# Keeping the two split parts of a mixer's weights in HBM for the second token half

## The chip, the cores and the metric

The kernel runs on one core of one Trainium2 chip. The metric is the device time of one execution in microseconds (us). A core has TensorE (PE: matmul, and PEld, its weight loads), VectorE (DVE), ScalarE (ACT), GpSimd (POOL) and SyncE (SP), each with its own queue of instructions that run in the order in which they stand. Before the change only SP issues DMAs; with it POOL does too.

## The reference

A trunk of two layers over 1024 tokens of 1024 features, all in float32. Layer 0 mixes tokens with a recurrent block, layer 1 with forgetting attention; beside each runs a cross-attention of four heads into 256 memory tokens. Then come an output projection and a squared-ReLU MLP.

```python
for layer in range(DEPTH):
    h = rms_norm(x, norm_mix[layer])
    if layer % N_MIXERS == 0:
        y_mix, xq = rglru_group(h, w_in_a[j], ...)   # proj = h @ w_in: u, gate, xq
    else:
        y_mix, xq = fox_group(h, w_in_b[j], ...)     # proj = h @ w_in: q, k, v, f, xq
    y_mem = memory_group(xq, mem, ...)
    x = x + jnp.concatenate([y_mix, y_mem], axis=-1) @ w_out[layer]
    x = x + sqrelu_mlp(rms_norm(x, norm_mlp[layer]), w_mlp_in[layer], w_mlp_out[layer])
```

## The kernel before

**Split weights.** Each float32 matrix product is made of three matmuls on rounded parts: a weight W is split into hi (W rounded, written by ACT) and lo (W minus hi, by DVE or POOL), an activation likewise, and the kernel adds hi·hi, hi·lo and lo·hi. `_wpart` is one such split of a piece of a tile. "Split" means this throughout.

**Weight tiles.** `self.plan` lists all weight tiles in the order of use. An entry is a source in HBM, a width (1024 columns, 512 KB; or 512 columns, 256 KB, a "half tile") and a number of pieces: 1 for tiles made by `plan_st`, 4 for tiles made by `plan_mv`. `_wraw` has SP load a tile into one of two raw buffers (`wr`), `_wsplit` splits it into one of three hi buffers (`wh`) and three lo buffers (`wl`); tile i uses buffer i mod 3. So tile i can be written when the last matmul of tile i-3 has run, and it must be there at its own first matmul. `pool_parts` says which of four pieces have their lo made by POOL; in the second token half of layer 1 it is all four.

**Two token halves.** Tokens are worked on in two halves of 512. In the mixers a weight tile is used for the first half, and much later the same tile is loaded and split again for the second. These are 60 entries: `wxqa` x4 and `wina` x8 (input projections of layer 0), `wout0` as 16 half tiles (output projection of layer 0), `wxqb` x4, `wkb`/`wqb` x8 and `wvb` x4 (projections of layer 1), `wout1m` x8 and `wout1x` x8 half tiles (output projection of layer 1). The MLP uses each weight once for both halves, and is not touched.

**Consumers.** `proj_T` uses one tile at a time (24 matmuls of 512 columns), `outproj` and `outproj2` a half tile (12 of 512 columns). `tok_proj` uses a pair of tiles: for each of four groups of 128 tokens 12 matmuls of 256 columns on the first tile of the pair, then 12 on the second, into one of two PSUM tiles `pspj`. A pair is asked for with `wpair`, which splits up to the tile behind the pair (`_wsplit(i + 3)`); so the second tile of each pair is written last, when the pair before is nearly used up.

**Order.** Python emits the instructions and weaves attention work between projections at fixed rates (`weave`); a scheduler of the framework then sets the order of each engine by its own estimate of times. Stores and loads of the residual stream (`xspill`) and of x stand on SP in the same queue as the weight loads. In the trace the second uses stand at 138 to 237 us (`wxqa`, `wina`), 305 to 353 (`wout0` halves), 1212 to 1402 (`wxqb`, `wkb`, `wqb`, `wvb`), 1455 to 1492 (`wout1m`) and 1535 to 1558 (`wout1x`); the first uses of the same at 5 to 138, 237 to 305, 1071 to 1180, 1180 to 1212 (`wout1m`) and 1411 to 1447 (`wout1x`).

Of the kernel before, what the change touches and what calls it, by code (L numbers as in the profile page):

```python
# [10 lines left out]
F32 = mybir.dt.float32  # L11
F32R = mybir.dt.float32r
# [7 lines left out]
P = 128  # L20
# [119 lines left out]
class Builder:  # L140
# [107 lines left out]
    def _wsplit(self, upto):  # L248
        nc = self.nc
        while self.wload < min(len(self.plan), upto):  # L250
            i = self.wload
            self._wraw(i + 1)
            n = self.plan[i][1]
            parts = self.plan[i][2]
            raw = self._wrawbuf(i)
            hi, lo = (self._wbuf(i, b) for b in (self.whi, self.wlo))
            if parts in ("s1", "s2"):
                G, q = nc.gpsimd, 256
                a11, a12, a22, a21 = (raw[:, k * q:(k + 1) * q] for k in range(4))
                f = self.F.get()  # L260
                if parts == "s1":
                    self.wx = f
                    G.tensor_tensor(f[:, q:2 * q], a21, a22, ALU.add)
                    G.tensor_tensor(f[:, 0:q], f[:, q:2 * q], a11, ALU.subtract)
                    self._wpart(hi[:, 0:512], lo[:, 0:512], raw[:, 0:512], nc.vector)
                    self._wpart(hi[:, 512:1024], lo[:, 512:1024], f[:, 0:512], nc.vector)
                else:
                    G.tensor_tensor(f[:, 0:q], a11, a21, ALU.subtract)
                    G.tensor_tensor(f[:, q:2 * q], a12, self.wx[:, 0:q], ALU.subtract)
                    self._wpart(hi[:, 512:768], lo[:, 512:768], a22, nc.vector)  # L270
                    self._wpart(hi[:, 0:512], lo[:, 0:512], f[:, 0:512], nc.vector)
# [184 lines left out]

    def plan_kv(self, l, idx=range(8)):
        for c in idx:
            self.plan.append((self.ins["wkv"][l * 8 + c], 1024, 4))

    def kv(self, l):
        nc = self.nc
# [574 lines left out]
    def plan_fox(self, c):  # L1037
        for w in ("wkb", "wqb"):
            self.plan_mv(w, (2 * c, 2 * c + 1))
        for kk in range(2):  # L1040
            self.plan.append((self.ins[f"wvb{c}"][kk], 1024 if c else 1056, 4))

    def fox_proj(self, h, c):
        nc = self.nc
# [222 lines left out]
    def run(self):  # L1267
        self.xs = self.dr.tile([8, P, S], F32, name="xspill")
        nc = self.nc
        xT = self.ins["xT"]  # L1270
        K_M, K_X, K_0, K_1 = [4, 5, 6, 7], [0, 1, 2, 3], [0, 1], [2, 3]

        self.plan.append((self.ins["wina"][0], 1024, 4))
        self.plan_st("wina", range(1, 4))
        for m in range(4):
            self.plan_kv(0, (2 * m, 2 * m + 1))
# [2 lines left out]
        self.plan_mv("wxqa")  # L1279
        self.plan_st("wina", range(8))  # L1280
        self.plan_st("wout0", range(8))
        w0 = self.ins["wout0"]
        self.plan += [(w0[m, :, 0:512], 512, 1) for m in range(7)]
        self.plan += [(w0[m, :, 512:1024], 512, 1) for m in range(7)]
        self.plan += [(w0[7, :, 0:512], 512, 1), (w0[7, :, 512:1024], 512, 1)]
        self.plan_mlp(0, 0, 0)
        self.plan_kv(1)
        self.plan_mv("wxqb")
        self.plan_fox(0)
        self.plan_fox(1)  # L1290
        self.plan += [(self.ins["wout1m"][m], 512, 1) for m in range(8)]
        self.plan_mv("wxqb")
        self.plan_fox(0)
        self.plan_fox(1)
        self.plan += [(self.ins["wout1x"][m], 512, 1) for m in range(8)]
        self.plan += [(self.ins["wout1m"][m], 512, 1) for m in range(8)]
        self.plan += [(self.ins["w1"][32 + m], 1024, 1) for m in range(TUNE["nz"])]
        self.plan += [(self.ins["wout1x"][m], 512, 1) for m in range(8)]
        self.plan_mlp(1, TUNE["nz"], TUNE["nw"])


        nrm = [self.norm_split_first(0, "gmix0", xT), self.norm_split(1, "gmix0", xT, True)]
# [231 lines left out]
```

## Time and profile before

| | |
|---|---|
| median of 3 runs | 2215.03 us (2212.84 to 2220.73) |
| the profiled execution | 2215.74 us, its span 2214.1 us |
| busy PE / DVE / ACT / POOL | 97% / 73% / 42% / 44% of the span |
| mean granted TensorE clock | 0.986 |
| moved by DMA | 307.85 MB, 139 GB/s on average |

Busy time is the share of the span in which an engine worked on an instruction. A wait is put down to the engine whose work came last. The granted clock is 1.00 at 2.4 GHz and 0.5 at 1.2 GHz; a value between is a mean over a stretch.

### The profile page before, as it was taken

To read this page: it belongs to the slowest core of one execution; us is meant where nothing else is said; L and a number is where in the kernel's file an instruction comes from. 1 tells how busy PE (TensorE), PEld (TensorE's weight loads), DVE (VectorE), ACT (ScalarE), POOL (GpSimd) and SP (SyncE) were. 2 spreads that over 40 slices of the span, in tenths; PEclk is the share of its full clock that TensorE was granted. 3 is DMA by queue.
4 is the path that set the end of the run, shared out by engine and by line. 5 is a ranking of instruction groups with operands and counts; after the bars stand their busy time and mean duration, and the time that the engine had idled before them with its cause. 6 is when DMAs were issued, how large, how long until landed. Compare 5 with 4: busy or idle time off the path is not lost. (4 is left out here: it accounts for less than half of the span.)

```text
span 2214.1 us, 31106 instructions
## 1 busy us (share of the span) xinstructions
PE 2138.4 (97%) x10662; PEld 1780.2 (80%) x10662; DVE 1617.9 (73%) x2991; ACT 932.4 (42%) x1852; POOL 983.2 (44%) x952
## 2 busy tenths in 40 slices
PE   7889999999999999998999998999999999999999
PEld 6788777888888888876998997777778888888887
DVE  8997776666666666669677877986787566576667
ACT  5755634222232222334556856765433223232222
POOL 3742421545545545456142452331364454454454
PEclk9989999999999999999999998999999999999999
DMA  5412254435445345345425221364564354354353
GB/s 177 129 58 67 93 178 157 134 123 190 138 129 190 130 136 183 126 134 166 125 87 172 96 73 49 125 193 129 168 209 167 104 187 159 107 190 151 108 194 128
DMA packets 138782, 307.85 MB, mean 139 GB/s; under 512 B 15552, under 2 KB 17664, under 8 KB 138624
## 3 DMA queue, kind: packets, MB, share of 16 engines
q1 hardware_dynamic: 138624, 305.87, 42.9%
q8 instruction: 84, 1.38, 0.3%
q14 instruction: 74, 0.61, 0.1%
HBM read 225.03 MB, written 80.77 MB: 138 GB/s over the span
## 5 line engine op out<-in xcount | busy, mean ns | idle before, releaser
L301 PE MATMUL pspj<-r,wh 128*128 128x512 f32 x2656 | 845.8, 398 | 15.5 <-ACT wh L245 5.6
L301 PEld LDWEIGHTS pspj<-r,wh 128*128 128x128 f32 x2656 | 498.4, 189 | 137.3 <-ACT wh L245 5.6
L301 PE MATMUL pspj<-r,wl 128*128 128x512 f32 x1328 | 528.4, 398 | 0.2 <-DVE wl L246 0.2
L245 ACT ACTIVATE wh<-wr 128x256 fp32r<-128x256 f32 (+3 forms) x497 | 275.3, 581 | 391.1 <-PE pspt L923 194.7
L246 DVE TENSOR_TENSOR wl<-wr,wh 128x256 fp32r<-128x256 f32 (+2 forms) x386 | 303.7, 794 | 67.7 <-ACT wh L245 66.7
L371 ACT ACTIVATE r<-f 128x512 fp32r<-128x512 f32 x250 | 156.8, 631 | 416.7 <-POOL f L881 278.4
L881 POOL TENSOR_TENSOR f<-f 128x512 f32<-128x512 f32 x128 | 167.6, 1310 | 320.0 <-DVE f L880 317.3
L301 PEld LDWEIGHTS pspj<-r,wl 128*128 128x128 f32 x1328 | 251.2, 189 | 60.9 <-DVE wl L246 0.7
L301 PE MATMUL pspj<-wh,r 128*128 128x256 f32 (+1 forms) x1408 | 275.5, 290 | 15.2 <-ACT f L450 5.1
L372 DVE TENSOR_TENSOR r<-f,r 128x512 fp32r<-128x512 f32 x250 | 190.3, 773 | 132.8 <-ACT r L371 132.6
L923 PE MATMUL pspt<-r,wh 128*128 128x512 f32 x768 | 246.8, 395 | 1.2 <-ACT f L948 1.0
L301 PEld LDWEIGHTS pspj<-wh,r 128*128 128x128 f32 x1408 | 225.9, 193 | 19.8 <-ACT f L450 6.0
L301 PE MATMUL pspj<-wl,r 128*128 128x256 f32 (+1 forms) x704 | 201.8, 288 | 5.0 <-DVE wl L246 5.0
L960 POOL TENSOR_TENSOR f<-f,f 128x512 f32<-128x512 f32 x64 | 96.3, 1505 | 230.8 <-DVE f L959 218.5
L923 PEld LDWEIGHTS pspt<-r,wh 128*128 128x128 f32 x768 | 144.1, 188 | 36.5 <-ACT wh L245 1.4
L923 PE MATMUL pss<-r,wh 128*128 128x512 f32 x512 | 161.6, 396 | 3.5 <-DVE f L968 3.5
L923 PE MATMUL pspj<-r,wh 128*128 128x512 f32 x512 | 161.2, 396 | 1.4 <-DVE f L949 1.2
L923 PE MATMUL pspt<-r,wl 128*128 128x512 f32 x384 | 152.4, 397 | 0.9 <-DVE wl L246 0.9
L246 POOL TENSOR_TENSOR wl<-wr,wh 128x256 fp32r<-128x256 f32 (+2 forms) x111 | 89.7, 831 | 132.5 <-ACT wh L245 129.0
L301 PEld LDWEIGHTS pspj<-wl,r 128*128 128x128 f32 x704 | 135.5, 193 | 6.7 <-DVE wl L246 5.8
L245 ACT ACTIVATE wh<-f 128x512 fp32r<-128x512 f32 x128 | 80.4, 630 | 143.2 <-PE pspj L923 61.3
L880 DVE SCALAR_TENSOR_TENSOR f<-pspj,f 128x512 f32<-128x512 f32 x128 | 87.7, 687 | 66.4 <-PE pspj L301 66.1
(273 smaller groups left out, 3635.5 us busy)
## 6 DMA issues: line engine op xcount, KB each, us to landing
f<-xspill SPq DMA_DIRECT2D x312, 256.0 KB, 3.0
xspill<-f SPq DMA_DIRECT2D x288, 256.0 KB, 3.0
wr<-in_w_dram SPq DMA_DIRECT2D x134, 512.0 KB, 4.1
f<-in_xT_dram SPq DMA_DIRECT2D x32, 256.0 KB, 3.7
wr<-in_wkv_dram SPq DMA_DIRECT2D x16, 512.0 KB, 3.9
wr<-in_wina_dram SPq DMA_DIRECT2D x15, 512.0 KB, 3.8
f<-cscr SPq DMA_DIRECT2D x24, 256.0 KB, 3.5
wr<-in_wxqa_dram SPq DMA_DIRECT2D x8, 512.0 KB, 3.8
```

Of the source, the lines that this page charges most:

```text
L245: self.nc.scalar.activation(hi, raw, AF.Copy)
L246: eng.tensor_tensor(lo, raw, hi.bitcast(F32), ALU.subtract)
L301: self.nc.tensor.matmul(out, lhsT=a, rhs=b, start=(j == 0), stop=(j == n - 1))
L371: self.nc.scalar.activation(hi[:, :n], src, AF.Copy)
L372: self.nc.vector.tensor_tensor(lo[:, :n], src, hi[:, :n].bitcast(F32), ALU.subtract)
L880: nc.vector.scalar_tensor_tensor(r[:, n], ps, 0.0, self.rsb[h][:, n], ALU.max, ALU.mult)
L881: nc.gpsimd.tensor_tensor(r[:, n], r[:, n], r[:, n], ALU.mult)
L923: nc.tensor.matmul(ps, lhsT=a, rhs=b, start=(j == 0), stop=(j == 5))
L960: G.tensor_tensor(c12, c12, u, ALU.add)
```

## The change

`share` goes over the plan. A full tile that is used again gets two tiles of its size in HBM (`wsp`, for hi and lo). At its first use, after the split, SP stores hi and lo there (104 stores: 36 tiles and 16 half tiles of two parts each). At its second use nothing is loaded to `wr` and nothing is split: POOL issues two DMAs, which bring hi and lo from HBM straight to the `wh` and `wl` buffers (120 DMAs for 60 entries). The 16 half tiles of `wout0` take their halves of the eight full tiles stored at the first use.

```diff
+    def ent(self, name, i, n, parts, a=0):
+        return (self.ins[name][i][:, a:a + n], n, parts, (name, i), a)
+
+    def share(self):
+        own, keep = {}, {}
+        for j, e in enumerate(self.plan):
+            if len(e) < 5:
+                continue
+            k, full = e[3], self.ins[e[3][0]].shape[2]
+            if k in own:
+                if k not in keep:
+                    keep[k] = [self.dr.tile([P, full], F32R, name=self.nm("wsp")) for _ in range(2)]
+                self.plan[j] = (None, e[1], "ld", k, e[4])
+            elif e[1] == full:
+                own[k] = j
+        self.own = {j: keep[k] for k, j in own.items() if k in keep}
+        self.keep = keep
...
-            if parts in ("s1", "s2"):
+            if parts == "ld":
+                _, _, _, k, a = self.plan[i]
+                for b, d in zip((hi, lo), self.keep[k]):
+                    nc.gpsimd.dma_start(b, d[:, a:a + n])
+            elif parts in ("s1", "s2"):
...
+                for b, d in zip((hi, lo), self.own.get(i, ())):
+                    nc.sync.dma_start(d.bitcast(F32), b.bitcast(F32))
...
-            self.plan.append((self.ins["wkv"][l * 8 + c], 1024, 4))
+            self.plan.append(self.ent("wkv", l * 8 + c, 1024, 4))
...
-        self.plan += [(w0[m, :, 0:512], 512, 1) for m in range(7)]
-        self.plan += [(w0[m, :, 512:1024], 512, 1) for m in range(7)]
-        self.plan += [(w0[7, :, 0:512], 512, 1), (w0[7, :, 512:1024], 512, 1)]
+        self.plan += [self.ent("wout0", m, 512, 1, a) for a in (0, 512) for m in range(7)]
+        self.plan += [self.ent("wout0", 7, 512, 1, a) for a in (0, 512)]
...
+        self.share()
```

The scheduler orders the engines anew. Three places show it. The first is PE in the second token half of layer 1, at the second tile of the pair `wqb` (the buffers `wh2_153` and `wl2_156`; the first tile of the pair is in `wh1_152` and `wl1_155`). Before, the 12 matmuls of a token group on the first tile are followed by its 12 on the second:

```order
L301 MATMUL pspj_840_11226<-wh1_152,r22_88 128x256
L301 MATMUL pspj_840_11226<-wl1_155,r22_88 128x256
L301 MATMUL pspj_840_11226<-wh1_152,r23_89 128x256
L301 MATMUL pspj_840_11226<-wh2_153,r18_84 128x256
L301 MATMUL pspj_840_11226<-wl2_156,r18_84 128x256
```

In the order of the change, the same place (`pspj_944` is the group that was `pspj_840`, and `pspj_946` the next group, in the other PSUM tile):

```order
L327 MATMUL pspj_946_11336<-wh1_152,r1_67 128x256
L327 MATMUL pspj_946_11336<-wh1_152,r22_88 128x256
L327 MATMUL pspj_946_11336<-wl1_155,r22_88 128x256
L327 MATMUL pspj_946_11336<-wh1_152,r23_89 128x256
L327 MATMUL pspj_944_11301<-wh2_153,r18_84 128x256
L327 MATMUL pspj_944_11301<-wl2_156,r18_84 128x256
```

The next group's 12 matmuls on the first tile moved ahead of the second tile's first matmul, and attention work moved between. From the last matmul of the buffer's old tile to the first on the new one there stood 24 matmuls of 256 columns and 3 of 128; now there stand 38 of 256, 12 of 128, 2 of 384 and 2 of 512.

The second place is POOL in the same stretch (`f` tiles times `frc` are softmax rows, `xr` the scaling of queries). Before:

```order
L1185 TENSOR_SCALAR f_127<-f_127,frc_10998 128x384
L246 TENSOR_TENSOR wl_156<-wr_150,wh_153 128x256
L1185 TENSOR_SCALAR f_144<-f_144,frc_11016 128x512
L246 TENSOR_TENSOR wl_156<-wr_150,wh_153 128x256 x2
L246 TENSOR_TENSOR wl_154<-wr_149,wh_151 128x264 x4
L246 TENSOR_TENSOR wl_155<-wr_150,wh_152 128x264 x4
```

In the order of the change:

```order
L1211 TENSOR_SCALAR f_127<-f_127,frc_11101 128x384
L280 DMA wl_156<-wsp_224 128x1024
L280 DMA wh_153<-wsp_223 128x1024
L1211 TENSOR_SCALAR f_144<-f_144,frc_11119 128x512
L280 DMA wl_154<-wsp_226 128x1056
L280 DMA wh_151<-wsp_225 128x1056
L280 DMA wl_155<-wsp_228 128x1056
L280 DMA wh_152<-wsp_227 128x1056
```

Four lo pieces of a tile became two DMA issues at the same place in POOL's queue.

The third place is SP where the half tiles `wout1m` are used first. Before:

```order
L241 DMA wr_149<-in_wout1m_dram 128x512
L794 DMA xspill<-f_127 128x512
L241 DMA wr_150<-in_wout1m_dram 128x512
L794 DMA xspill<-f_134 128x512
L241 DMA wr_149<-in_wout1m_dram 128x512
L400 DMA f_134<-xspill 128x512
```

In the order of the change:

```order
L261 DMA wr_149<-in_wout1m_dram 128x512
L302 DMA wsp_247<-wh_153 128x512
L820 DMA xspill<-f_127 128x512
L302 DMA wsp_248<-wl_156 128x512
L261 DMA wr_150<-in_wout1m_dram 128x512
L302 DMA wsp_249<-wh_151 128x512
L820 DMA xspill<-f_134 128x512
L302 DMA wsp_250<-wl_154 128x512
L261 DMA wr_149<-in_wout1m_dram 128x512
L426 DMA f_134<-xspill 128x512
```

Two stores of parts now stand ahead of each weight load, and so ahead of the `xspill` loads and stores that follow.

## Rows read from the trace of the kernel before

**Rows 1.** The page: span, and busy us (share) of each engine.

```profile
span 2214.1 us, 31106 instructions
...
PE 2138.4 (97%) x10662; PEld 1780.2 (80%) x10662; DVE 1617.9 (73%) x2991; ACT 932.4 (42%) x1852; POOL 983.2 (44%) x952
```

**Rows 2.** Waits of PE: for whom, us in total, times, longest.

```profile
PE pspj L301 <- ACT wh L245: 5.6, 1, 5.6
PE pspj L301 <- DVE wl L246: 5.2, 4, 2.7
PE pspj L301 <- ACT f L450: 5.1, 4, 1.9
PE pspt L301 <- DVE wl L246: 4.6, 1, 4.6
```

**Rows 3.** Stretches: us, busy (instructions) by engine, PE clock, DMA share, GB/s.

```profile
core 0: us, PE busy (x) PEld busy (x) DVE busy (x) ACT busy (x) POOL busy (x), PEclk, DMA share, GB/s
64.00:138.00 74.00, 61.03 (x375) 55.57 (x374) 70.24 (x123) 49.82 (x106) 48.90 (x42) 0.86 0.32 93
138.00:237.00 99.00, 97.13 (x584) 84.87 (x583) 77.38 (x159) 55.43 (x120) 32.04 (x40) 1.00 0.23 70
237.00:305.00 68.00, 60.81 (x267) 48.92 (x266) 56.18 (x82) 38.90 (x76) 30.27 (x27) 0.92 0.42 134
305.00:328.00 23.00, 21.46 (x96) 16.90 (x95) 12.48 (x28) 7.31 (x13) 2.69 (x2) 1.00 0.58 187
328.00:353.00 25.00, 25.00 (x109) 20.19 (x108) 19.03 (x29) 14.90 (x23) 0.00 (x0) 1.00 0.68 215
1071.00:1180.00 109.00, 109.00 (x906) 107.88 (x905) 77.53 (x221) 60.77 (x165) 36.16 (x46) 1.00 0.30 91
1180.00:1212.00 32.00, 31.52 (x168) 26.22 (x166) 22.39 (x55) 18.27 (x43) 7.49 (x11) 1.00 0.62 181
1212.00:1238.00 26.00, 21.74 (x143) 19.39 (x144) 20.92 (x54) 21.55 (x55) 8.37 (x13) 0.93 0.47 163
1238.00:1345.00 107.00, 104.46 (x853) 102.30 (x853) 80.80 (x235) 65.95 (x185) 55.75 (x84) 1.00 0.26 78
1448.00:1493.00 45.00, 41.97 (x227) 34.57 (x226) 39.15 (x104) 30.37 (x69) 15.66 (x20) 1.00 0.61 187
1535.00:1559.00 24.00, 23.49 (x102) 18.34 (x101) 19.51 (x29) 13.57 (x23) 1.04 (x1) 1.00 0.50 171
```

**Rows 4.** Groups by shape, ACT, DVE, POOL: the splits (busy us, mean ns, idle before).

```profile
L245 ACT ACTIVATE wh<-wr 128x256 fp32r<-128x256 f32 x276 | 101.2, 410 | 66.3 <-PE pspt L923 22.9 <-DMA wr<-in_wkv_dram 17.6 <-PE pspj L301 15.6
L245 ACT ACTIVATE wh<-wr 128x1024 fp32r<-128x1024 f32 x93 | 98.5, 1059 | 166.8 <-PE pspt L923 111.9 <-PE pspj L301 28.7 <-DMA wr<-in_w_dram 17.8
L245 ACT ACTIVATE wh<-wr 128x512 fp32r<-128x512 f32 x112 | 70.3, 629 | 158.1 <-PE pspj L301 72.6 <-PE pspt L923 59.9 <-DMA wr<-in_wout1x_dram 7.4
...
L246 DVE TENSOR_TENSOR wl<-wr,wh 128x1024 fp32r<-128x1024 f32 x93 | 123.8, 1332 | 18.3 <-ACT wh L245 18.2
...
L246 DVE TENSOR_TENSOR wl<-wr,wh 128x512 fp32r<-128x512 f32 x111 | 87.9, 792 | 30.4 <-ACT wh L245 30.0
...
L246 POOL TENSOR_TENSOR wl<-wr,wh 128x256 fp32r<-128x256 f32 x98 | 79.5, 832 | 121.1 <-ACT wh L245 117.6 <-PE pspt L1210 3.4
```

**Rows 5.** The page: DMA queue share, and issues (count, KB, median us to landing).

```profile
q1 hardware_dynamic: 138624, 305.87, 42.9%
...
f<-xspill SPq DMA_DIRECT2D x312, 256.0 KB, 3.0
...
wr<-in_w_dram SPq DMA_DIRECT2D x134, 512.0 KB, 4.1
...
wr<-in_wxqa_dram SPq DMA_DIRECT2D x8, 512.0 KB, 3.8
```

**Rows 6.** DMA view: half tiles of layer 1's output projection.

```profile
wr<-in_wout1m_dram SPq DMA_DIRECT2D x16, 256.0 KB, 2.9
```

**Rows 7.** Waits of ACT from 1205 to 1230 us.

```profile
ACT r L365 <- DMA f<-xspill: 5.2, 4, 2.0
```

More of the change, by code (lines that the diff above doesn't have):

```diff
@@ L642, in plan_st @@
         for i in idx:
-            self.plan.append((self.ins[name][i], 1024, 1))
+            self.plan.append(self.ent(name, i, 1024, 1))
     def plan_mv(self, name, idx=range(4)):
         for i in idx:
-            self.plan.append((self.ins[name][i], 1024, 4))
+            self.plan.append(self.ent(name, i, 1024, 4))
     def proj_T(self, xs, tag="pj"):
@@ L1040, in plan_fox @@
         for kk in range(2):
-            self.plan.append((self.ins[f"wvb{c}"][kk], 1024 if c else 1056, 4))
+            self.plan.append(self.ent(f"wvb{c}", kk, 1024 if c else 1056, 4))
     def fox_proj(self, h, c):
@@ L1271, in run @@
         K_M, K_X, K_0, K_1 = [4, 5, 6, 7], [0, 1, 2, 3], [0, 1], [2, 3]
-        self.plan.append((self.ins["wina"][0], 1024, 4))
+        self.plan.append(self.ent("wina", 0, 1024, 4))
         self.plan_st("wina", range(1, 4))
@@ L1281, in run @@
         self.plan_st("wout0", range(8))
-        w0 = self.ins["wout0"]
-        self.plan += [(w0[m, :, 0:512], 512, 1) for m in range(7)]
-        self.plan += [(w0[m, :, 512:1024], 512, 1) for m in range(7)]
-        self.plan += [(w0[7, :, 0:512], 512, 1), (w0[7, :, 512:1024], 512, 1)]
+        self.plan += [self.ent("wout0", m, 512, 1, a) for a in (0, 512) for m in range(7)]
+        self.plan += [self.ent("wout0", 7, 512, 1, a) for a in (0, 512)]
         self.plan_mlp(0, 0, 0)
@@ L1290, in run @@
         self.plan_fox(1)
-        self.plan += [(self.ins["wout1m"][m], 512, 1) for m in range(8)]
+        self.plan += [self.ent("wout1m", m, 512, 1) for m in range(8)]
         self.plan_mv("wxqb")
@@ L1294, in run @@
         self.plan_fox(1)
-        self.plan += [(self.ins["wout1x"][m], 512, 1) for m in range(8)]
-        self.plan += [(self.ins["wout1m"][m], 512, 1) for m in range(8)]
+        self.plan += [self.ent("wout1x", m, 512, 1) for m in range(8)]
+        self.plan += [self.ent("wout1m", m, 512, 1) for m in range(8)]
         self.plan += [(self.ins["w1"][32 + m], 1024, 1) for m in range(TUNE["nz"])]
-        self.plan += [(self.ins["wout1x"][m], 512, 1) for m in range(8)]
+        self.plan += [self.ent("wout1x", m, 512, 1) for m in range(8)]
         self.plan_mlp(1, TUNE["nz"], TUNE["nw"])
+        self.share()
         nrm = [self.norm_split_first(0, "gmix0", xT), self.norm_split(1, "gmix0", xT, True)]
```

## The prediction

> **What bounds the kernel now.** I read the page first, then the waits of PE, then a table of stretches of the mixers. PE is busy for 97% of the span, DVE for 73%, ACT and POOL for under half [rows 1]. So only what PE waits for can be won back: 2214.1 - 2138.4 = 76 us in all. The waits of PE say on whom: of the splits only a few, 5.6 us for hi (the start of the program), 5.2 and 4.6 us for lo [rows 2]. The lo waits lie nearly all between 64 and 138 us, where DVE works 70.2 of 74 us [rows 3]. That is a first use, and the change leaves its split as it is.
>
> The stretches of the second uses are the ones to price. PE idles there 99.0 - 97.1 = 1.9 us (138 to 237), 1.5 (305 to 328), 0 (328 to 353), 4.3 (1212 to 1238), 2.5 (1238 to 1345), 3.0 (1448 to 1493) and 0.5 (1535 to 1559): 13.7 us together [rows 3]. The clock is 1.00 in all but one of them: 0.93 from 1212 to 1238, worth 0.07 x 26 = 1.8 us. So about 15.5 us is the most that the change can give.
>
> **What is removed.** By the plan 60 splits go: on ACT 32 pieces of 512 columns at 0.629 us, 8 of 1024 at 1.059, 80 of 256 at 0.410, about 61 us; on POOL 62 lo pieces of about 0.83, 51 us (counted in the two orders); on DVE 32 at 0.79, 8 at 1.33 and 18 short ones, some 45 us [rows 4]. All of it lies beside PE's work. It pays only where ACT or DVE is what PE waits for. I take 2 us of the 4.3 at 1212 to 1238, 2 of the 3.0 at 1448 to 1493 and 1 of the 1.5 at 305 to 328: **-5**, with bounds 0 and -15.5.
>
> **What is added: the reloads.** A tile is now two DMAs that POOL issues when the buffer's old tile is used up. Most have room: counted in the changed order, PE has 10 to 20 us of matmuls between the old tile's last and the new one's first for `wina` and for the first tile of most pairs. Room is short at the second tile of a pair. A matmul of 256 columns costs PE 109.0/906 = 0.12 us, one of 512 25.0/109 = 0.229 [rows 3]; I take 0.06 for 128 and 0.172 for 384 in proportion. At `wqb`'s second tile the order before leaves 24 x 0.12 + 3 x 0.06 = 3.1 us, the changed one 38 x 0.12 + 12 x 0.06 + 2 x 0.172 + 2 x 0.229 = 6.1 us. The nine places of this kind, in program order, have 4.5, 6.5 (`wxqa`), 6.8 (`wxqb`), 6.7, 6.1, 5.8, 6.5, 4.8 and 7.5 us (`wkb` to `wvb`). The scheduler has made room, but not much.
>
> The price of a reload is not in the trace, since nothing is issued from POOL. The nearest row is a 512 KB load from SP: 3.8 to 4.1 us to landing [rows 5]. The second part shares the engines with the first: 305.87 MB in 42.9% of 2214.1 us is 322 GB/s with all engines busy [rows 5], so 0.524 MB more is 1.6 us. For POOL's work on an issue I take that of a short POOL piece, 0.83 us [rows 4], twice. Together 4.0 + 1.6 + 1.6 = 7.2 us. Below, the second part and the issues could cost nothing: 4.1. Above, one part after the other: 2 x 4.1 + 2 x 0.83 = 9.9. I take 7.2, since transfers in flight together are what the kernel's SP loads do all the time. Against the nine rooms that leaves 2.7 + 0.7 + 0.4 + 0.5 + 1.1 + 1.4 + 0.7 + 2.4 + 0 = **+9.9** us; at 4.1 nothing; at 9.9 it is 33.9.
>
> The Trainium skill (DMA: Bandwidth & Descriptors, Anatomy of one DMA) gives a DMA issued from GpSimd about 2.0 us plus its bytes at 436 GB/s, so an estimate of 4.4 us for both parts issued together. By that estimate this term would be 0. No row here has a DMA from POOL, and for the same bytes the rows from SP are slower than this formula (3.8 to 4.1 us against 3.2), so I keep the rows.
>
> Half tiles: two parts cost 2.9 [rows 6] + 0.8 + 1.6 = 5.3 us. PE has 12 x 0.229 x 2 = 5.5 us between for some 20 of the 32, which just covers it, more for the others, and 3.2 us for one `wout1x` tile: **+2**. At the upper price of 2 x 2.9 + 1.7 = 7.5 us three buffers give a tile each (7.5 + 2.75)/3 = 3.4 us in place of 2.75, so 20 x 0.67 = 13 us.
>
> A POOL DMA that waits for PE's last matmul holds POOL's queue; behind it stand softmax rows (`frc`) for the attention's transposes. Before, the lo pieces stood in the same places and waited for the same release, so this is new only as far as PE itself is late. Nothing is added for it.
>
> **What is added: the stores.** 36 x 2 x 0.524 + 16 x 2 x 0.262 = 46 MB go out, and 46 MB of reloads come in, in place of 23 MB of loads. Taken as engine time at 322 GB/s: from 1071 to 1180, 16 tiles of 1.05 MB are 52 us of 109, which makes a DMA share of 0.30 + 0.48 = 0.78; from 237 to 305, 8.4 MB are 26 us of 68: 0.42 + 0.38 = 0.80; from 1180 to 1212, 4.2 MB are 13 us of 32: 0.62 + 0.41 = 1.03; and the reloads' extra 0.26 MB for nine half tiles from 328 to 353 make 0.68 + 0.29 = 0.97 [rows 3]. Two stretches are full. An excess of 0.03 x 32 is 1 us; the loads behind it on SP's queue are those of the residual stream, for which ACT waits 5.2 us already from 1205 to 1230 [rows 7]. I take **+2**, with bounds 0 and 13: at the upper one each of eight pairs of stores holds up the loads behind it for its own 0.52 MB, 1.6 us. Elsewhere the cover is the 0.2 and more of idle DMA share; if it were gone, the same 1.6 to 3.3 us a tile would show.
>
> **The clock.** Where PE idles 7.2 us with waits of 3.4 and 3.2 us, from 237 to 305, the granted clock is 0.92, between its two levels of 1.2 and 2.4 GHz, which costs 0.08 x 68 = 5.4 us; in stretches with 1.5 to 3.0 us of idle time it stays at 1.00 [rows 3]. Two of the new stalls are over 2 us. I take **+2**; were all 33.9 us to come, 5.4/7.2 of it would be 25.
>
> **The sum.** -5 + 9.9 + 2 + 2 + 2 = +11 on the profiled execution's own 2215.74 us (span 2214.1; the median of the runs is 2215.03, so it is a usual one): 2226.7 against it, 2226 against the median.
>
> **The rivals.**
> *The reload is dear.* One part comes after the other, or POOL is slow to issue: 9.9 us and 7.5 us. Then +33.9 + 13, with 2 to 13 for stores and about half of the clock's upper bound, less 5: 2262 to 2285, or some 2250 if only the full tiles suffer. For it speaks that no row shows POOL doing this; against, that the scheduler left 5 to 7 us where 3 to 4 stood. It decides from 8 us on. The Trainium skill (SBUF — State Buffer, Who interferes with whom) adds that GpSimd cannot write descriptors while DVE runs a one-source copy or scalar operation in SBUF. No run here shows it yet. As a mechanism of this kernel, an issue that has to let one DVE instruction end first waits 0.8 to 1.3 us, as long as DVE's pieces are [rows 4]: nine times at most 12 us, so some 2238, which the forecast's own range holds.
> *The cover holds, nothing is won.* A reload takes 6 us or less; what ACT and DVE no longer do was hidden. Sum -2 to +2: 2213 to 2218. For it speaks PE's 97%.
> *Faster.* Reloads fit as in the last case, and PE's idle time in the second uses goes with the splits: up to -15.5 + 2, so 2202. It is decided from 1212 to 1238, where ACT works 21.6 of 26 us and DVE 20.9 [rows 3]; the waits there must be for ACT's queue. Against it: part of them is for the residual stream [rows 7], which the stores make later.
> *The stores hold SP.* +13 from 1180 to 1238 and some as much again from 237 to 305, where each store pair is 1.05 MB: 2235 to 2245, with reloads fitting.
>
> **Chances.** Forecast (2214 to 2240) 0.42; dear reload 0.18; nothing won 0.17; faster 0.13; stores 0.10. A measurement of this kernel tells about 0.5%, 11 us, from no change: faster means under 2204, slower over 2226. Half of the forecast's case lies beyond that line: slower 0.21 + 0.18 + 0.10 = 0.49; same 0.21 + 0.15 = 0.36; faster 0.13 + 0.02 = 0.15. The range 2202 to 2262 leaves out the dear half of the first rival and the best end of the third, under 2 in 10.
>
> **What would show it.** In the changed profile: ACT and POOL busy time down by some 61 and 50 us, and DVE's by 45. PE waits for POOL DMAs into `wh` or `wl` at the second tiles of pairs, most at `wxqa` and the last `wqb` pair. The time from issue to landing in the list of DMA issues is the price itself: under 5 us for 512 KB, the nine stalls are gone; over 8, the first rival holds. The stretch from 1180 to 1238 shows the stores: a DMA share near 1 and longer waits for `xspill`. I am wrong if PE's waits do not change and the time still does, or if the attention's work, which the scheduler moved into the gaps, makes PE wait for DVE in new places.

## The result and the profile after

| | before | changed |
|---|---|---|
| median of 20 runs each | 2215.12 us (2212.46 to 2220.73) | 2219.34 us (2215.00 to 2226.76) |
| ratio, 95% interval | | 1.0019 [1.0012, 1.0025] |
| span of the profiled execution | 2214.1 us | 2220.3 us |

The change costs 4.2 us, 0.2%. That is on the side that was forecast, inside the range and 6.7 us under the forecast of 2226; it lies within the 0.5% that the prediction called no change. The profiled execution lost 6.2 us.

The head of the changed kernel's page, span and busy times, answers to [rows 1]:

```profile
span 2220.3 us, 31077 instructions
...
PE 2136.6 (96%) x10662; PEld 1775.3 (80%) x10662; DVE 1566.7 (71%) x2933; ACT 881.8 (40%) x1732; POOL 1006.5 (45%) x1010
```

DVE is down by 51 us and ACT by 51, POOL is up by 23, and PE's own work is the same to 2 us. So the 6 us, and two more, are idle time of PE: span less busy time is 75.7 us before and 83.7 now. Which waits of PE are new (engine, line, waited for: us in total, times, longest) answers to [rows 2]:

```profile
PE pspj L327 <- ACT wh L265: 7.7, 3, 5.6
...
PE pspt L1236 <- DVE r L1169: 5.0, 1, 5.0
...
PE pspj L327 <- ACT r L397: 2.7, 1, 2.7
...
PE pss L844 <- DMA wl<-wsp: 1.7, 1, 1.7
PE pspj L844 <- DMA wh<-wsp: 1.4, 1, 1.4
...
PE pspj L327 <- DMA wh<-wsp: 0.6, 1, 0.6
```

The reloads themselves (`wsp`) stop PE for 1.7 + 1.4 us at half tiles of `wout0` and 0.6 us at the last pair of `wvb`, 3.7 us in all. Two other waits, of 5.0 and 2.7 us, each happen once. Where they are, a table of stretches of the changed kernel tells; it is cut where PE has done the same work as at 138.5, 236.6, 304.9 us and so on in the trace before, and one row (1204 to 1222) is a close-up. It answers to [rows 3]:

```profile
core 0: us, PE busy (x) PEld busy (x) DVE busy (x) ACT busy (x) POOL busy (x), PEclk, DMA share, GB/s
135.20:233.60 98.40, 95.89 (x578) 83.74 (x577) 68.08 (x147) 46.76 (x108) 36.22 (x54) 1.00 0.44 148
233.60:302.00 68.40, 60.81 (x268) 48.60 (x267) 55.55 (x80) 36.05 (x71) 34.23 (x32) 0.93 0.69 234
302.00:366.00 64.00, 59.29 (x260) 47.06 (x259) 27.02 (x51) 18.22 (x27) 18.27 (x30) 1.00 0.79 243
1072.00:1181.00 109.00, 108.20 (x897) 106.87 (x896) 76.84 (x218) 60.59 (x165) 36.23 (x46) 1.00 0.68 242
1181.00:1210.50 29.50, 29.50 (x154) 24.73 (x152) 19.22 (x49) 14.64 (x34) 6.82 (x13) 1.00 0.90 294
1204.00:1222.00 18.00, 10.96 (x57) 8.90 (x56) 9.59 (x23) 7.09 (x16) 4.21 (x8) 0.86 1.06 352
1210.50:1265.30 54.80, 44.89 (x324) 42.27 (x323) 33.44 (x92) 34.88 (x81) 12.32 (x22) 0.91 0.50 167
1265.30:1351.00 85.70, 85.69 (x696) 83.87 (x695) 57.81 (x194) 37.95 (x105) 30.87 (x51) 1.00 0.46 144
1351.00:1404.70 53.70, 49.02 (x280) 39.77 (x278) 44.97 (x138) 39.68 (x98) 18.44 (x28) 0.90 0.17 55
...
1497.20:1535.00 37.80, 37.31 (x189) 30.52 (x187) 23.11 (x47) 19.13 (x39) 13.68 (x16) 1.00 0.61 198
1535.00:1563.80 28.80, 25.71 (x105) 19.92 (x104) 18.82 (x28) 13.50 (x22) 6.41 (x11) 0.94 0.56 162
```

From 1265.3 to 1351 us, where five of the nine feared tiles stand, PE is idle for 0.01 us; before, the same work (1258.0 to 1344.1) had 2.5 us of idle time. From 1210.5 to 1265.3, the four tiles of `wxqb`, PE idles 9.9 us and the clock is 0.91; before, this took 47.0 us (1211.0 to 1258.0), 4.4 of them idle, at 0.96. That is 7.8 us lost in one place. From 1535 to 1563.8 PE idles 3.1 us at 0.94; before, it was 23.6 us with 0.3 us idle: 5.2 us more. The stretch ahead of it takes 37.8 us where it was 42.1 (1492.5 to 1534.6), 4.3 us less, so that the two together lose 0.9.

**What holds PE at 1212 us.** Rows of the changed kernel's timeline, ACT, DVE and PE (start us, us, engine, line, in brackets the idle time before and what ended it):

```profile
1214.28 0.72 ACT L391 ACTIVATE r<-f,par 128x512 fp32r<-128x512 f32 x1 [5.85 <-DMA f<-xspill]
1215.03 0.68 ACT L1168 ACTIVATE r<-pspt,gk 64x512 fp32r<-64x512 f32 x1
1215.04 0.75 DVE L392 SCALAR_TENSOR_TENSOR r<-f,par,r 128x512 fp32r<-128x512 f32 x1 [5.60 <-ACT r L391]
...
1216.42 0.76 DVE L1169 SCALAR_TENSOR_TENSOR r<-pspt,gk,r 64x512 fp32r<-64x512 f32 x1
...
1217.23 0.69 PE L1236 MATMUL pspt<-ident,f 128*128 128x128 f32 x2 [5.04 <-DVE r L1169]
...
1218.22 0.72 ACT L391 ACTIVATE r<-f,par 128x512 fp32r<-128x512 f32 x1 [2.51 <-DMA f<-xspill]
...
1218.99 0.58 PE L327 MATMUL pspj<-wh,r 128*128 128x256 f32 x1 [1.07 <-ACT r L391]
```

ACT waits 5.85 us for a block of the residual stream from HBM (`f<-xspill`). Behind that wait on ACT's queue stands L1168, and behind the same block on DVE's queue L1169, both for the attention; PE waits for L1169. The waits view names DVE, but what is late is a DMA. The place of L1168 in ACT's order costs little by itself: once L1169 is done, PE has two matmuls left (0.7 us) and then stands again, for the next block of the residual stream (ACT's L391 at 1218.22), which the first projection of the second half reads. That block was issued at 1207.43 us and landed at 1218.20, after 10.8 us; in the kernel before it took 7.3 (1205.53 to 1212.81). The DMA view of 1204 to 1222 us says why (share of the 16 engines by queue, then KB each and median us from issue to landing):

```profile
q0 software_dynamic: 864, 3.15, 53.5%
q1 hardware_dynamic: 1756, 3.20, 52.7%
issues: line engine op xcount, KB each, median us to landing
wh<-wsp POOLq DMA_DIRECT2D x3, 512.0 KB, 7.2
wl<-wsp POOLq DMA_DIRECT2D x3, 512.0 KB, 8.6
f<-xspill SPq DMA_DIRECT2D x6, 256.0 KB, 9.4
```

The DMA engines are full (1.06 in the table; the share counts the time of packets, and it can pass 1). At the end of the first half of the last output projection the three weight buffers come free one after the other, POOL issues the parts of three `wxqb` tiles from 1203.7 to 1212.5 us, 3.15 MB, and just then SP fetches the residual stream for the second half. A load that lands in 3.1 us as a rule takes 9.4. The stretch was crowded before the change too; the same views of the kernel before:

```profile
1204.00:1222.00 18.00, 15.17 (x88) 12.18 (x87) 15.08 (x35) 13.07 (x32) 6.24 (x10) 1.00 0.85 268
...
f<-xspill SPq DMA_DIRECT2D x7, 256.0 KB, 6.3
```

So the loads went from 6.3 to 9.4 us here, and PE's idle time from 2.8 to 7.0. POOL's queue (q0) and SP's (q1) get half of the engines each, and a load that POOL issued later, at 1208.37 us, was in at 1215.62 although it is twice as large as the block that SP had issued at 1207.43. The Trainium skill (DMA: Bandwidth & Descriptors, Queues, rings and completion order) says that each DMA engine goes round the queues that have work, a packet at a time; 53.5% against 52.7% agrees with it.

What a reload cost, and what POOL's issues cost, from the page's list of DMA issues and from the groups by shape (these answer to [rows 5] and [rows 4]):

```profile
wl<-wsp POOLq DMA_DIRECT2D x26, 512.0 KB, 4.7
wh<-wsp POOLq DMA_DIRECT2D x26, 512.0 KB, 5.7
...
wh<-wsp POOLq DMA_DIRECT2D x32, 256.0 KB, 4.2
wl<-wsp POOLq DMA_DIRECT2D x32, 256.0 KB, 4.6
```

Of a full tile POOL mostly issues the lo part first (18 of 26, among them the nine feared ones), as here for the second tile of a pair:

```profile
1329.14 0.58 POOL L280 DMA_DIRECT2D wl<-wsp  x1 [0.83 <-PE pspj L327]
1329.72 0.54 POOL L280 DMA_DIRECT2D wh<-wsp  x1
```

So the first part lands 4.7 us after its own issue and the second 5.7 after its own; both are in 6.3 us after the first issue (median of the 26; 5.2 us for the half tiles).

```profile
L266 POOL TENSOR_TENSOR wl<-wr,wh 128x256 fp32r<-128x256 f32 x44 | 40.0, 928 | 88.1 <-ACT wh L265 80.3 <-DMA wr<-in_wvb_dram 7.7
...
L280 POOL DMA_DIRECT2D wh<-wsp x60 | 33.0, 550 | 60.5 <-PE pspj L327 35.4 <-PE pspt L844 11.3 <-PE pss L844 9.8
```

### The profile page after: what moved, and what is told of

It is laid out like the page before. It is cut to its first block, busy times and chain, and to the rows that moved or that the text cites. A ratio compares the mean times of both kernels' runs of the same rounds, so it can differ in the third digit from the quotient of the medians.

```text
span 2220.3 us, 31077 instructions
## 1 busy us (share of the span) xinstructions
PE 2136.6 (96%) x10662; PEld 1775.3 (80%) x10662; DVE 1566.7 (71%) x2933; ACT 881.8 (40%) x1732; POOL 1006.5 (45%) x1010
## 5 line engine op out<-in xcount | busy, mean ns | idle before, releaser
L265 ACT ACTIVATE wh<-wr 128x512 fp32r<-128x512 f32 (+3 forms) x377 | 218.2, 604 | 362.4 <-PE pspt L949 191.2
L397 ACT ACTIVATE r<-f 128x512 fp32r<-128x512 f32 x250 | 156.5, 631 | 423.1 <-POOL f L907 274.8
L266 DVE TENSOR_TENSOR wl<-wr,wh 128x256 fp32r<-128x256 f32 (+3 forms) x328 | 257.4, 792 | 50.3 <-ACT wh L265 49.8
L265 ACT ACTIVATE wh<-f 128x512 fp32r<-128x512 f32 x128 | 80.4, 630 | 144.5 <-PE pspj L949 64.7
L1211 POOL TENSOR_SCALAR f<-f,frc 128x512 f32<-128x512 f32 (+2 forms) x96 | 61.5, 651 | 154.1 <-DVE frc L1209 123.0
```

The costliest lines, as they stand in the source:

```text
L265: self.nc.scalar.activation(hi, raw, AF.Copy)
L266: eng.tensor_tensor(lo, raw, hi.bitcast(F32), ALU.subtract)
L397: self.nc.scalar.activation(hi[:, :n], src, AF.Copy)
L1211: nc.gpsimd.tensor_scalar(s[:, :n], s[:, :n], rc, 0.0, ALU.mult, ALU.add)
```

## The experiments

Theory A after the first look: the loss is made in the second mixer, by reloads that fill the DMA engines while the residual stream is due, and by the end of the last `wout1x` tiles. Theory B, the rival that the prediction named: the stores do it. Theory C: the split was never in the way, and only the order of the work moves the time. Fourteen kernels were run, each against the kernel before on the same chip, most with 11 runs (e2 has 5, e10 has 6). The last column is the ratio's distance from 1 times 2215 us; by it the changed kernel stands at +4.2.

| run | what goes through HBM | median us | ratio, 95% interval | in us |
|---|---|---|---|---|
| e1 | first mixer alone | 2212.67 | 0.9991 [0.9982, 1.0000] | -2.0 |
| e2 | second mixer alone | 2222.35 | 1.0036 [1.0022, 1.0050] | +8.0 |
| e3 | stores alone, nothing reloaded | 2215.87 | 1.0002 [0.9991, 1.0013] | +0.4 |
| e4 | all, a quarter of each `wxqb` part reloaded | 2208.91 | 0.9978 [0.9969, 0.9988] | -4.9 |
| e5 | all but `wxqb` | 2216.54 | 1.0005 [0.9995, 1.0015] | +1.1 |
| e6 | all but `wout1m`, `wout1x` | 2216.55 | 1.0011 [1.0002, 1.0020] | +2.4 |
| e7 | all, reloads issued by SP | 2215.69 | 1.0000 [0.9991, 1.0009] | 0.0 |
| e8 | first mixer, `wkb`, `wqb`, `wvb` | 2210.28 | 0.9979 [0.9970, 0.9987] | -4.7 |
| e9 | as e5, 16 idle POOL DMAs more | 2210.74 | 0.9978 [0.9968, 0.9989] | -4.9 |
| e10 | as e8, reloads issued by SP | 2205.72 | 0.9960 [0.9945, 0.9975] | -8.9 |
| e11 | `wxqb` alone | 2214.99 | 1.0001 [0.9991, 1.0010] | +0.2 |
| e12 | `wkb`, `wqb`, `wvb` alone | 2209.29 | 0.9974 [0.9965, 0.9983] | -5.8 |
| e13 | all, `wxqb` reloaded by SP | 2213.36 | 0.9996 [0.9987, 1.0005] | -0.9 |
| e14 | all but `wout1x` | 2213.83 | 0.9997 [0.9988, 1.0007] | -0.7 |

Where each kernel stands against the kernel before, in us, at PE's last matmul on the tile named (its time in the trace, less that of before; one execution each, and two executions of the same order differ by 2 to 3 us):

| PE's last matmul on | before, at | changed | e4 | e6 | e11 | e12 | e13 | e14 |
|---|---|---|---|---|---|---|---|---|
| `wxqa`, second use | 169.8 | -2.8 | -2.5 | -2.1 | +0.6 | +0.9 | -1.8 | -2.4 |
| `w1` tile 1, layer 0 | 378.2 | 0.0 | +2.6 | -2.8 | +2.5 | +0.4 | -3.1 | -1.5 |
| `wout1m`, first use | 1211.0 | -0.5 | +3.3 | -1.2 | +2.3 | +1.2 | -3.0 | -1.0 |
| `wxqb`, last tile, second use | 1258.0 | +7.3 | -0.1 | +3.6 | +5.0 | -2.5 | +1.8 | +7.4 |
| `wqb`, last tile, second use | 1344.1 | +6.7 | -0.4 | +4.1 | +1.0 | -3.0 | +0.7 | +7.1 |
| `wvb`, last tile, second use | 1402.5 | +2.1 | -6.9 | +0.6 | +1.3 | -8.0 | -5.1 | +2.0 |
| `w1` tile 3, early, layer 1 | 1534.6 | +0.3 | -10.7 | -0.1 | -1.5 | -10.4 | -7.8 | -1.3 |
| `wout1x`, second use | 1558.2 | +5.6 | -3.9 | -0.2 | -1.2 | -10.2 | -3.0 | 0.0 |
| the end | 2209.5 | +6.1 | -4.2 | -0.7 | +0.4 | -10.4 | -2.8 | -0.2 |

**e1 and e2: the two mixers apart.**

```diff
-            if len(e) < 5:
+            if len(e) < 5 or not (j < 60):      # e1; in e2 (j > 60)
```

> Only the weights of the first mixer (wxqa, wina, wout0) go through HBM; the second mixer splits twice as before. Theory A (the loss arises in the second mixer alone, where the first reloads of wxqb fill the DMA engines while the residual stream is due): no change, 2213 to 2217 us, since the two traces stand level again at 365 us. Theory B (the stores cost time wherever they are made): half of the loss or more shows here, 2217 us or more. Theory C (the split was never in the way and nothing but the order moves the time): within 2 us of before as well.

> Only the weights of the second mixer (wxqb, wkb, wqb, wvb, wout1m, wout1x) go through HBM. Theory A: all of the loss is here, 2218 to 2221 us, with the same 5 us gap of PE near 1215 us and the same gap near 1542 us as in the changed kernel. Theory B: about half of it, some 2217 us. If the two halves of the change depend on each other, the time is neither.

PE's order in e1 is the changed kernel's in the first mixer and the old one in the second, and the reverse in e2. The first mixer wins 2.0 us (its interval just reaches 0), the second loses 8.0: theory A has the place right, and both times fall a little outside the ranges that it gave. In e2's trace the gap of PE stands at 1219 us (5.2 us), and the one of 2.7 us at 1544.

**e3: the stores alone.**

```diff
-                self.plan[j] = (None, e[1], "ld", k, e[4])
```

> Both parts of each tile are stored at first use, and the second use loads the weights and splits them as before: 46 MB of stores are added and nothing is taken away. Theory A: the stores are hidden, 2214 to 2217 us, and PE's waits at the start of the second token half of the second mixer (1211 to 1258 us) stay as before. Theory B: the stores push the residual stream's loads back on SP's queue, 2219 us or more, with a longer wait of ACT for xspill.

46 MB of stores cost 0.4 us, with an interval from -2.0 to +2.9. From 1205 to 1240 us ACT waits 1.7 us for `xspill`, less than before [rows 7]. Theory B falls as the only cause. PE's order differs here too, in 1,712 of 10,612 matmuls, and the time does not move, which speaks against theory C as far as this order goes.

**e4: fewer bytes in the reloads of `wxqb`.**

```diff
+                c = 256 if k[0] == "wxqb" else n
                 for b, d in zip((hi, lo), self.keep[k]):
-                    nc.gpsimd.dma_start(b, d[:, a:a + n])
+                    nc.gpsimd.dma_start(b[:, :c], d[:, a:a + c])
```

> The reloads of wxqb alone fetch 256 of the 1024 columns of each part (the rest of the buffer keeps old values, so a part of the weights is left out of the computation); everything else is the changed kernel, and PE's order differs from it only in the stretch from 1206 to 1299 us. Theory A: the DMA engines are no longer full from 1204 to 1220 us, ACT waits for xspill no longer than before (5 us in place of 8), the 5 us gap of PE goes; up to 8 us less than the changed kernel where nothing later takes it back, 2211 to 2216 us. Theory B and C: 2218 to 2221 us, the gap stays.

Where the changed kernel is at +4.2 us, this one is at -4.9: 9 us go with the bytes of four tiles. The DMA engines are still busy from 1204 to 1222 us, at 0.97 (that part of the expectation was wrong), but the residual stream lands in 5.2 us and PE's longest gap there is 1.5 us:

```profile
1204.00:1222.00 18.00, 15.69 (x92) 13.30 (x91) 13.61 (x30) 10.70 (x23) 5.39 (x10) 1.00 0.97 299
```

The block that holds PE in the changed kernel stands at the same place in SP's order here and lands 5.5 us after its issue (1211.53 to 1217.01) in place of 10.8. So theory A holds for the landing. Theory C is not wholly out: PE's order is the changed kernel's except from 1206 to 1299 us (507 of 10,612 matmuls), and ACT's L1168 stands ahead of the residual blocks in e4, as it does before. By the rows at 1218 us that order is worth little, but no run separates it.

**e5 and e6: one group of tiles taken back.**

```diff
-            if len(e) < 5:
+            if len(e) < 5 or not (e[3][0] != "wxqb"):      # e5
+            if len(e) < 5 or not (not e[3][0].startswith("wout1")):      # e6
```

> wxqb alone is split twice as before; all other repeated tiles go through HBM, and the computation is whole. Theory A (reload burst): at the start of the second token half of the second mixer the loads of wxqb are half as many bytes again, PE's 5 us gap at 1215 us goes, and the 10 us that the changed kernel loses from 1211 to 1245 us mostly stay away: 2209 to 2214 us. Rival (the loss there is one of the order in which the scheduler put the work, or of POOL's queue, and not of bytes): 2217 us or more.

> wout1m and wout1x are split twice as before; the mixers' other tiles go through HBM. PE's order is that of the kernel before from 1425 us on. Theory A says nothing is won at 1215 us (the three reloads of wxqb are the same), but the 2.7 us gap near 1542 us and the slow clock behind it belong to the order of the last wout1x tiles and go: up to 5 us less than the changed kernel, 2213 to 2218 us. If the stores of wout1m ahead of 1210 us feed the burst, the gap at 1215 us shrinks too and the time is below 2212 us.

e5's median misses theory A's 2209 to 2214. Its trace says why: in e5 the `xspill` loads from 1204 to 1222 us land in 4.3 us and PE's longest gap from 1205 to 1225 us is 1.1 us; PE does its last matmul at 2206.1 us, 3.4 before the kernel before, and yet the span is 2217.4. The 11.3 us between are a last DRAIN of POOL of 10.5 us, behind which the program ends (e9). In e6 the gap near 1542 us is gone, as theory A said, and the gap of 5.0 us becomes two of 2.6, which points to a share of the stores of `wout1m`, though the order of the work differs there as well; PE ends 0.7 us ahead of the kernel before. A DRAIN of 8.6 us covers this up: the span ends 8.7 us after PE in place of 4.6.

**e9: the last DRAIN.** The kernel is e5's with one line more in the split of the MLP's tiles, taken for the first 16 of them:

```diff
+            self.nc.gpsimd.dma_start(t, f[:, 0:16])      # t: a tile in HBM, not read
```

> The kernel of e5 (wxqb split twice, all other tiles through HBM, 112 DMAs issued by POOL) and 16 DMAs more from POOL of 8 KB each (16 columns of an intermediate of the first MLP block go to a scratch tensor that nobody reads); the order of PE's instructions is that of e5 to the last one. In e5 the program does not end until a last DRAIN of POOL of 10.5 us is over, against 1.4 us without POOL DMAs and 2.5 us in the changed kernel with its 120; with 56, 64, 80, 88 and 112 it is 1.37 us + 0.082 us for each. Theory: that DRAIN is work left over from the DMAs that POOL issued, and beyond some number between 112 and 120 most of it is done earlier. Then more DMAs make the program shorter: a DRAIN of 2 to 4 us and 2208 to 2212 us. Rival: the DRAIN grows with each one (12 us) or has nothing to do with their number: 2215 to 2219 us.

The DRAIN falls to 3.2 us and the time from +1.1 to -4.9 us, with more DMAs and PE's order unchanged. Over all kernels (number of DMAs that POOL issues; the DRAIN, and from PE's last matmul to the span's end, us):

```
kernel    before e3   e7   e10  e11  e12  e1   e2   e8   e6   e5    changed e4   e9   e13  e14
DMAs      0      0    0    0    8    24   56   64   80   88   112   120     120  128  128  128
DRAIN     1.37   1.38 1.37 1.38 2.05 3.35 5.96 6.62 7.92 8.58 10.54 2.54    2.54 3.20 3.18 3.20
PE to end 4.57   4.52 4.63 4.53 4.33 4.69 6.52 7.01 8.64 8.73 11.28 4.69    4.34 4.69 4.84 4.34
```

From 8 to 112 DMAs it is 1.37 us + 0.082 us for each, to 0.03 us; at 120 and 128 the step is again 0.082, but some 106 DMAs have dropped out. Up to about 3.5 us are hidden behind the output's last stores. The changed kernel, with 120, happens to pay nothing; e5 pays 6.7 us, e6 and e8 4.1, e2 2.4 and e1 1.9 (from the last row, less 4.6). Without that e1 and e2 stand at -3.9 and +5.6, together +1.7, against +4.2 for the whole change; the intervals of the two are 2 and 3 us to either side.

**e7 and e13: the other queue.** In e7 SP issues all reloads, in e13 those of `wxqb` alone (with 16 idle POOL DMAs, as in e9):

```diff
-                    nc.gpsimd.dma_start(b, d[:, a:a + n])
+                    nc.sync.dma_start(b.bitcast(F32), d[:, a:a + n].bitcast(F32))
```

> The same reloads are issued by SP in place of POOL, on the queue of the residual stream. Theory A (bytes on the engines): DMA is as full from 1204 to 1220 us, the loss there stays, 2217 to 2226 us, more where a reload that waits for its buffer holds the loads behind it. Rival (a second queue takes the engines from the first; in one queue a load that is issued earlier is served earlier): the gap near 1215 us shrinks to 2 us or less, 2209 to 2216 us.

> The changed kernel with the eight reloads of wxqb issued by SP in place of POOL, on the queue of the residual stream (and 16 idle DMAs of 8 KB from POOL in the first MLP block, so that the last DRAIN stays short); PE's order is the changed kernel's but for 238 places between 1206 and 1290 us. Theory A1 (the engines serve POOL's queue and SP's by turns, so a load of the residual stream that was issued first gives half of its engine time away to the reloads): on one queue the loads of xspill land in 7 us or less in place of 9.4, PE's gap near 1215 us falls from 5 us to 2 or less, time 2211 to 2216 us. Theory A2 (only the sum of bytes counts): the gap stays at 4 to 5 us, 2217 to 2222 us.

e13 is at -0.9 us, 5 us under the changed kernel, with the same bytes in the same stretch. In one queue `xspill` lands in 7.5 us in place of 9.4, and from 1204 to 1222 us PE idles 2.4 us in place of 7.0 (longest gap 2.3; A1's 7 and 2 us are narrowly missed):

```profile
1204.00:1222.00 18.00, 15.56 (x83) 13.67 (x82) 11.48 (x32) 9.96 (x25) 2.91 (x6) 0.81 0.96 337
```

So the landings agree with A1: in e13 the loads of `xspill` come in by their order of issue, 7.2 to 7.7 us after it, where the five issued from 1206 to 1209 us in the changed kernel take 8.0 to 12.5. That the other queue alone gives the 5 us is not shown. In e13 SP also fetches the block that holds PE first (issued at 1204.21, landed at 1211.38), ahead of another block and a load of `cscr` that precede it in the changed kernel. e7, where SP fetches that block first as well, shows the same at 1213 us (7.4 us to landing, a gap of 2.1), and its time is at the upper end of the rival's range that was named there.

**e11 and e12: one part alone.**

```diff
-            if len(e) < 5:
+            if len(e) < 5 or not (e[3][0] == "wxqb"):      # e11
+            if len(e) < 5 or not (e[3][0][:2] in ("wk", "wq", "wv") and e[3][0] != "wkv"):      # e12
```

> Only wxqb goes through HBM, all else is split twice. Theory A (burst): the loss at 1211 to 1245 us is there without the later gains: 3 to 8 us over the kernel before, 2218 to 2223 us, with ACT waiting 8 us for xspill. If the stores of wout1m, which are not there, are what fills the engines as much as the reloads do: 2213 to 2217 us.

> Only wkb, wqb and wvb go through HBM, reloaded from POOL (24 DMAs). Theory A: the gain of some 5 to 7 us from 1245 to 1402 us shows alone, nothing is lost at 1211 us or from 1535 us on, the last DRAIN (3.3 us by the rule of e9) stays hidden: 2207 to 2211 us. If the gain of e8 came from the first mixer's tiles: 2213 to 2216 us.

e11's time is that of the case in which the stores of `wout1m` count as much. By itself the burst costs 2.7 us from 1211 to 1258 us (+2.3 to +5.0 in the table, `xspill` landing in 8.0 us), where the changed kernel loses 7.8, and e6, which doesn't store `wout1m`, 4.8. By 1344 us 4 of e11's 5.0 us are gone again: from 1258.0 to 1344.1 PE idles 2.5 us before, and a PE that comes late idles 0.4 us there, which is 2 of the 4. So theory A's 3 to 8 us were too much for this part alone. It looks as if reloads and stores make the loss together (the orders of the work differ too), and part of a loss ahead of 1344 us is not paid.

e12 is at -5.8 us: the reloads of the pairs win by themselves. Three rows of e12, cut at nearly the same work, show where:

```profile
1212.20:1255.50 43.30, 40.92 (x314) 38.17 (x314) 32.47 (x93) 34.43 (x88) 15.43 (x24) 1.00 0.44 148
1255.50:1341.10 85.60, 85.17 (x695) 83.36 (x694) 58.44 (x193) 38.50 (x105) 30.56 (x50) 1.00 0.46 145
1341.10:1394.50 53.40, 45.72 (x282) 36.32 (x280) 45.24 (x138) 39.23 (x97) 18.48 (x28) 1.00 0.12 38
```

Before, this took 47.0, 86.1 and 58.4 us. PE's idle time falls by 2.0 and 2.1 us in the first two (from 4.4 and 2.5). The second has 13 matmuls more than before and the third 14 fewer, so these two are best taken together: 139.0 us where it was 144.5. In the third PE's idle time is 7.7 us where it was 6.3, but the clock is 1.00 where it was 0.88, worth an estimated 0.12 x 58.4 = 7.0 us; in the changed kernel it is 0.90 there. This is one execution, 3.6 us under e12's own median.

**e14: the last tiles.**

```diff
-            if len(e) < 5:
+            if len(e) < 5 or not (e[3][0] != "wout1x"):
```

> The changed kernel with wout1x split twice (and 24 idle DMAs of 8 KB from POOL in the first MLP block, so that the last DRAIN stays short). PE's order is the changed kernel's up to 1420 us and differs by 62 places from 1504 to 1572 us. Theory: the 2.7 us gap at 1542 us and the slow clock behind it come with the reloaded wout1x, whose last tiles the scheduler put ahead of the end of the attention; here the gap goes and PE ends 3 to 6 us earlier; the loss at 1211 us stays as it is: 2213 to 2217 us. Rival (the end of the attention is late for another reason, such as the loss at 1211 us): the gap stays, 2218 to 2221 us.

At -0.7 us it is 4.9 us under the changed kernel (24 idle POOL DMAs, as in e9, are in it as well). The gap at 1217 us is still there (5.9 us), the one of 2.7 us is 1.0 us, and the clock from 1535 to 1565 us is 1.00:

```profile
PE pspj L335 <- ACT r L405: 1.0, 1, 1.0
```

e2, e4 and e13, which reload `wout1x`, have the 2.7 us gap whatever happens at 1211 us. So the gap comes with the reloaded `wout1x`. How is argued from PE's order and not tested: the scheduler puts early MLP tiles and `wout1x` matmuls ahead of the attention's end (the 4.3 us won from 1497 to 1535), and then PE has nothing left to do while the last attention rows go through ACT and DVE (`r` of L397): the time won is lost again, with an estimated 0.06 x 28.8 = 1.7 us of slow clock.

**e8 and e10: what is worth keeping.**

```diff
-            if len(e) < 5:
+            if len(e) < 5 or not (j < 60 or e[3][0][:2] in ("wk", "wq", "wv")):
```

> Through HBM go the first mixer's tiles and wkb, wqb, wvb of the second; wxqb, wout1m and wout1x are split twice. Theory A with the account by stretches (reloads from 1245 to 1402 us win some 7 us, the burst at 1211 us and the tail from 1535 us lose 10 and 5): faster than before by 3 to 8 us, 2206 to 2211 us. If the 7 us are only what PE catches up after the burst, they do not show where there is no burst: 2212 to 2216 us.

> The kernel of e8 (the first mixer's tiles and wkb, wqb, wvb through HBM) with the reloads issued by SP. Theory on the DRAIN: it is 1.4 us again, the program ends 4.6 us after PE as in the kernel before, not 8.7 us, and the time falls by up to 4 us below e8: 2204 to 2209 us. Rival: on SP's queue a reload that waits for its buffer holds the residual stream's loads, PE's waits grow and the gain goes: 2211 us or more.

e8 leaves out the groups that lose and is at -4.7 us. e10 issues its reloads from SP as in e7, which takes the DRAIN away as well: 2205.72 us, 0.9960 [0.9945, 0.9975], 8.9 us faster than the kernel before and 13 than the changed one. The DRAIN is 4.1 us of what separates the two (8.64 against 4.53 in the table), so no gain of the queue itself shows here, and the intervals of e8 and e10 touch. Its page:

```profile
span 2204.8 us, 31043 instructions
...
PE 2133.4 (97%) x10662; PEld 1774.7 (80%) x10662; DVE 1580.2 (72%) x2957; ACT 895.5 (41%) x1764; POOL 951.7 (43%) x898
```

## Why the prediction was right in direction and wrong in its terms

The sum +11 came out as +4.2 (+6.2 in the profiled execution), but hardly by its own terms.

- **The reloads at the nine pairs, +9.9: the step that failed.** Measured: PE waits 0.6 us for `wsp` there, once, at the last pair of `wvb`. The price was set at 7.2 us from release to both parts landed, against rooms of 4.5 to 7.5 us counted in matmuls. From PE's last matmul on the old tile to both parts landed it was 5.4 to 6.6 us at eight of the nine and 8.2 at the last, median 6.2. The 1.6 us for the second part was right (6.3 - 4.7 above); mis-sized were the two issues, put on top as 2 x 0.83 us: an issue takes 0.55 us, and the first one lies inside the time to landing. The rooms were off as well: PE came to the new tile after 6.6 and 5.5 us where 4.5 and 4.8 had been counted, and 6.2 us against the counted rooms would still have left 3.6. The margin was thin. At four of the nine PE's first matmul on the tile starts 0.04 us after the landing, so a reload that is a microsecond dearer would have been paid there. By the Trainium skill's formula for a DMA from GpSimd (DMA: Bandwidth & Descriptors, Anatomy of one DMA) both parts were an estimate of 4.4 us and the term 0: the landing is nearly 2 us above it, and its verdict on these rooms was the better one.
- **The rival of the dear reload.** Its range, 2262 to 2285, does not come out of its terms: 33.9 + 13 + 2 to 13 + 12.5 - 5 gives 2271 to 2282. The Trainium skill (SBUF — State Buffer, Who interferes with whom) names issues held up while DVE runs in a two-port mode; 120 issues between 0.527 and 0.732 us show no delay of a DVE instruction's length. Whether DVE was in such a mode no run tells.
- **What a reload does to the loads beside it, not in the sum: +7.8 us at one place.** The prediction saw full engines at 1180 to 1212 us (estimate 1.03; measured 0.90 from 1181 to 1210.5, and 1.06 from 1204 to 1222) and a late residual stream, but laid it to the stores and priced it at +2. The rival "the stores hold SP" had the place, nearly twice the size (+13 from 1180 to 1238) and the wrong culprit: e3 clears the stores alone, and e4 shows that it is the bytes of the reloads, twice those of the old loads, let go where three buffers come free within 9 us. By e13's landings the second queue makes those loads later still; how much of PE's loss is due to that, and how much to the order of SP's loads, stays open. The stores seem to feed it where both are there (e11 and e6 against the changed kernel).
- **The gain, -5: too small.** e12 alone gives -5.8 us, e10 -8.9. The 15.5 that were set as the most left out a second use, 1344 to 1402 us: 6.3 us of idle time and a clock of 0.88, just where e12's trace wins most (58.4 to 53.4 us). From 1212 to 1256 us 2.0 us of idle time are won there, where 2 were put, and 2.1 at the later pairs, for which nothing was put.
- **Half tiles, +2: near.** The price was 5.3 us, and 5.2 was measured. The waits of PE for `wsp` at `wout0`'s halves are 1.7 and 1.4 us, and the stretch from 302 to 366 us is 3.9 us longer than before. `wout1x` was said to be short of room; only weight loads wait there, 0.5 us, and the scheduler's new order at 1535 us, which the prediction named only as what could make it wrong, cost 5 us, 4.3 of which had been won just ahead.
- **Stores, +2: 0.4 us (e3).** Hidden where nothing else is added.
- **Clock, +2: both signs.** From 1210.5 to 1265.3 us it costs an estimated 0.09 x 54.8 = 4.9 us, against 0.04 x 47.0 = 1.9 before; where there is no such stall it gives up to 7 us back (e12).
- **Busy times.** DVE and ACT fell by 51 each (45 and 61 were said), the lo pieces on POOL by 45; but POOL rose by 23 us, since 120 issues of 0.55 us count as its work, 66 us. The text priced them and then forgot them in its check.

"Cover holds, nothing is won" came nearest in time and was not what happened: about 9 us were there to be won (e10). In the trace 7.8 us are lost from 1211 us, 3.9 at the half tiles and 5.2 at 1535, and 4.7 are won back from 1351 to 1404.7 and 4.3 from 1497 to 1535. That the total lies so near to zero, and inside the range, is luck: the largest term of the sum hardly came, and a loss that was not in it came in its place.

Open: why the clock stays at 1.00 in e12 and falls to 0.88 before with as much idle time from 1344 us on; why an order of the scheduler's that was good for one tile group was bad for the next; whether one queue would help without the new order of SP's loads. The sizes by stretch are from one execution each.

## What to carry to other kernels

A transfer that fits its own buffer's room is not yet free: look at which other load is due while it runs, above all where several buffers come free together, and which engine queue stands behind that load. Replace a computation by a transfer group by group, keep the groups that win (here the paired tiles), and watch which queue the transfers take: from another queue they can overtake loads that are urgent (that one queue is faster for that reason alone is not shown here). When a median and PE's last matmul disagree, read the end of the program.

## What the runs showed of the hardware

- A program in which POOL issues DMAs ends with a DRAIN of POOL of 1.37 us + 0.082 us for each (8 to 112 DMAs, up to 10.5 us); with 120 and 128 it is 2.5 and 3.2 us. Sixteen useless DMAs made e5 6 us faster.
- Issued from POOL, a 512 KB reload takes POOL 0.55 us. Of two issued together the first lands in 4.7 us, the second in 5.7 after its own issue, both 6.3 us after the first (medians); in the full stretch from 1204 to 1222 us the medians are 7.2 and 8.6.
- Two queues with work shared the DMA engines in halves (53.5% and 52.7%): 512 KB that POOL issued at 1208.37 us landed at 1215.62, ahead of 256 KB that SP had issued at 1207.43 (1218.20). In one queue the loads of `xspill` came in by their order of issue (median 7.5 against 9.4 us).
- The clock from 1341 to 1394 us stayed at 1.00 in e12 with 7.7 us of PE idle, and was 0.88 before with 6.3.
